# A decoder trunk on one core: the items of an attention head on 13 slots, and the projection's weight buffers opened inside the gate

## The chip, the cores and the metric

The kernel runs on one NeuronCore of a Trainium2 chip. The metric is the device time of one execution in microseconds. The engines are TensorE (PE in the profile, its weight loads PEld), VectorE (DVE), ScalarE (ACT), GpSimd (POOL), and SyncE (SP), which issues every DMA of this kernel.

## The reference, cut to what matters

Two layers work on 512 tokens of width 2048. Layer 0 is a pooling mixer, layer 1 sparse attention: an indexer scores the keys of each query, the best 128 are kept (as an additive mask here), and 16 heads of width 128 attend with it.

```python
proj = h @ w_in
q, k, v, gate, qi, ki, wi = jnp.split(proj, ATTN_SPLITS, axis=-1)
q = rope_partial(q.reshape(B, L, N_HEADS, HEAD_DIM), positions, ROT_DIM)
k = rope_partial(k.reshape(B, L, N_HEADS, HEAD_DIM), positions, ROT_DIM)
...
logits = jnp.einsum('bqhd,bqkhd->bhqk', qb, k_sel).astype(jnp.float32) * attn_scale
logits = jnp.where(valid[:, None], logits, -jnp.inf)
p = jax.nn.softmax(logits, axis=-1).astype(v.dtype)
return jnp.einsum('bhqk,bqkhd->bqhd', p, v_sel)
...
return (o * jax.nn.silu(gate)) @ w_out
```

Every layer's input is RMS-normed and modulated, its output is scaled by a gate from the conditioning vector and added to the residual.

## The kernel before

**Products.** All matmuls are of fp32r. An operand is split into a rounded part (ScalarE casts it, `hi`, `wh`, `qwh`) and the remainder (VectorE subtracts, `lo`, `wl`, `qwl`), and each product is three matmuls: hi·hi, hi·lo, lo·hi. So each unit of weights costs a load, a cast and a subtraction before TensorE can take it. `gemm_t` and `gemm_n` loop over eight steps `kp` of 256 rows of the contraction.

**Order of the work.** It is written out by hand. Two queues of closures hold the work beside the matmuls: `hot` and `bg`. After each step, `step(n, nhot)` runs `nhot` items of `hot` and, by a running debt, on average `n` items of `bg`; `mid={n: f}` calls f after the matmuls of step n, ahead of that `step`; `drain()` runs all that is left. The order in the program is a priority: the framework then lays down one fixed order for each engine, in which work that it expects to be ready can come ahead of earlier work that it expects to wait. A tile in a pool opened with `reuse_waits="tile"` waits for the readers of those tiles that lay at its place before.

**The gate.** After the indexer's projection, four chunks `c` of the gate are multiplied (L715, `gemm_t` over eight steps of 24 matmuls each, banks `acc`). `gate_evac` applies SiLU on ScalarE into `yst` (four buffers, in pool `yp`) and stores it to `yd` in DRAM. Meanwhile `bg` holds 8 `s_item` (sums and differences of `hT` into `SS`) and 54 top-k items (L655 on), which work on `score` in pool `ip`. Then `drain()` runs what is left of them, `yp`, `ip`, the work pools and the banks are closed, and the projection's pools `ap`, `wq` (its buffers `qst` x4, `qwh` x4, `qwl` x4, `t2` x4) and banks are opened.

**The projection.** For each pair of heads a = 2j, b = 2j+1, seven products P1 to P7 of a Strassen-like scheme replace eight: 28 slots `u` of 12 matmuls each (128x384), over the banks `bx`, `bz`, `by`. `qplan` orders them: slots 0 to 11 run P1, P5, P6 in turn, 12 to 19 P3 and P7, 20 to 27 P2 and P4. `q_unit` prepares the weights of a slot: it issues the loads up to `QAHEAD` = 2 units ahead, forms the sums that P5, P6, P7 and P4 need with VectorE (L760), and splits; it runs until `QLOOK` + 1 = 4 units are ready. After P7's last slot (19) the 11 items of head b are put on `bg`, after P4's last (27) those of head a, and each slot ends with `step(1)`: one item a slot. The first pair's slots also take 8 `s3_item` (differences of `hT`).

**The items of a head** (`head_items`): `rot_qk` rotates q and k (VectorE, last write L546), `turned` transposes q, then k (TensorE L825, cast, remainder), `keep_v` splits v and loads the stored gate, `soft(qb)` computes the scores of a block of queries (L849 to L851), adds the mask and takes the maximum (VectorE L854), and the exponential (ScalarE L857); `norm_p` divides (VectorE L863), `trans` transposes the probabilities (TensorE L869, cast and remainder into `ph`, `pl`), `pvs` multiplies by v (L880 to L882) and by the gate (L883). The PSUM tag `att`, which `turned`, `soft`, `trans` and `pvs` share, has two banks here. `vh`, `vl`, `ph`, `pl`, `na`, `nb` are single buffers.

**After the projection**, the first gemm of the output (L961) runs with `nstep=2.6, nhot=2, mid={6: drain}`; meanwhile the last items, and `y_split` for the 16 heads, come from `hot` and `bg`. Its step `kp` reads `yT` of heads 2kp and 2kp+1; the last pair is heads 14 (a) and 15 (b).

Of the kernel before, what the change touches and what calls it, by code (L numbers as in the profile page):

```python
# [9 lines left out]
F32 = mybir.dt.float32  # L10
# [4 lines left out]
PSUM = bass.MemoryType.PSUM  # L15
# [3 lines left out]
T = 512  # L19
# [14 lines left out]
NS = 3.4  # L34
NC = 1
# [19 lines left out]
def trunk(ctx, tc, xT, cols, crow, pos, modT, win, wgrp, wout0, widx, wgate, wqkv, wout1, out):  # L55
# [6 lines left out]
    P = {}  # L62
# [16 lines left out]
    ew = open_work("left")  # L79
    eb = open_banks()  # L80
# [53 lines left out]
    def drain():  # L134
        while hot:
            hot.popleft()()
        while bg:
            bg.popleft()()
# [41 lines left out]
    def gemm_t(kps, rhs, new_bank, evac, t0=0, t1=T, nstep=1, nhot=1, mid={}):  # L180
        banks = []
        for n, kp in enumerate(kps):
            wh, wl = next_unit()
            for m in range(4):
                if n == 0:
                    banks.append(new_bank())
                o = banks[m][:, 0:t1 - t0]
                for kk in range(2):
                    rh, rl = rhs(2 * kp + kk)
                    ms = slice(m * 128, m * 128 + 128)  # L190
                    first = n == 0 and kk == 0
                    last = n == len(kps) - 1 and kk == 1
                    mm(o, wh[:, kk, ms], rh[:, t0:t1], start=first, stop=False)  # L193
                    mm(o, wh[:, kk, ms], rl[:, t0:t1], start=False, stop=False)  # L194
                    mm(o, wl[:, kk, ms], rh[:, t0:t1], start=False, stop=last)  # L195
                if n == len(kps) - 1:
                    evac(m, o)
            if n in mid:
                mid[n]()
            step(nstep, nhot)  # L200
# [99 lines left out]
    hT = {}  # L300
# [22 lines left out]
    es = ExitStack()  # L323
# [128 lines left out]
    for g in range(4):  # L452
        pooled = {}
        for kk in range(4):
            k = 4 * g + kk
# [98 lines left out]

    er = ExitStack()
    sp = er.enter_context(tc.tile_pool(name="sp", bufs=1, side="right"))
    es = ExitStack()
    yp = es.enter_context(tc.tile_pool(name="yp", bufs=1))
    ip = es.enter_context(tc.tile_pool(name="ip", bufs=1))
# [12 lines left out]
    y = {}  # L572

    def y_tile(m):
        y[m] = yp.tile([128, T], F32, name="yst", tag="yst", bufs=4)

    for m, o in early_g:
        y_tile(m)
# [127 lines left out]
    def gate_evac(c, t0):  # L706
        def evac(m, o):
            mt = 4 * c + m
            if mt not in y:
                y_tile(mt)  # L710
            nc.scalar.activation(y[mt][:, t0:T], o, AF.Silu)
            nc.sync.dma_start(yd[mt], y[mt])
        return evac

    for c in range(4):  # L715
        t0 = 256 if c == 0 else 0
        gemm_t(range(8), lambda k: hT[k], bank4, gate_evac(c, t0), t0, T, nstep=NS if c > NC else 0.5)
    drain()
    es.close()
    ew.close()  # L720
    eb.close()

    QW = 384
    el = ExitStack()
    ap = el.enter_context(tc.tile_pool(name="ap", bufs=1, reuse_waits="tile"))
    wq = er.enter_context(tc.tile_pool(name="wq", bufs=1, side="right", reuse_waits="tile"))
    eq = ExitStack()
    P["ps"] = eq.enter_context(tc.tile_pool(name="pq", bufs=1, space=PSUM, reuse_waits="tile"))
    P["natt"] = 2


    qplan = []
# [21 lines left out]
    def q_unit():  # L754
        i = qpos[1]
        qpos[1] += 1
        q_loads(i + 1 + QAHEAD)
        prod, kp, _ = qplan[i]
        st = qraw.pop(i, None)
        sub = lambda o, x, z: nc.vector.tensor_tensor(o, x, z, op=OP.subtract)  # L760
        if prod == "P5":
            sub(st, st, was["b11"])
        elif prod == "P6":
            t2[kp] = wq.tile([128, 2, QW], F32, name=f"t2_{kp}")
            sub(t2[kp], st, was["t1"])
            st = t2[kp]
        elif prod == "P7":
            sub(st, was["b22"], st)
        elif prod == "P4":
            sub(t2[kp], was["b21"], t2[kp])  # L770
            st = t2[kp]
        keep = {"P1": "b11", "P5": "t1", "P3": "b22", "P2": "b21"}.get(prod)
        if keep:
            was[keep] = st
        wh = wq.tile([128, 2, QW], F32R, name="qwh", tag="qwh", bufs=QLOOK + 1)
        wl = wq.tile([128, 2, QW], F32R, name="qwl", tag="qwl", bufs=QLOOK + 1)
        split(wh, wl, st)
        qready.append((wh, wl))

    def lhs(prod, k, tt):  # L780
        ts = slice(tt * 128, tt * 128 + 128)
# [36 lines left out]
    def head_items(h, nat):  # L818
        x = nat.rearrange("p t (o d) -> p t o d", o=3)
        cell = {}  # L820

        def turned(s, nm):
            p = att()
            for tt in range(4):
                nc.tensor.transpose(p[:, tt * 128:tt * 128 + 128], x[:, tt, s, :], ident)  # L825
            a = ap.tile([128, T], F32R, name=nm + "h", tag=nm + "h")
            b = ap.tile([128, T], F32R, name=nm + "l", tag=nm + "l")
            split(a, b, p)
            cell[nm] = (a, b)

        def rot_qk():
            rope(ap, "rh", x[:, :, 0:2, 0:32], cosa, sina, [128, 4, 2, 32], 16)

        def keep_v():
            vh = ap.tile([128, 4, 128], F32R, name="vh", tag="vh")
            vl = ap.tile([128, 4, 128], F32R, name="vl", tag="vl")
            split(vh, vl, x[:, :, 2, :])
            cell["v"] = (vh, vl)
            cell["ph"] = ap.tile([128, 4, T], F32R, name="ph", tag="ph")
            cell["pl"] = ap.tile([128, 4, T], F32R, name="pl", tag="pl")  # L840
            cell["y"] = ap.tile([128, T], F32, name="yg", tag="yg", bufs=2)
            nc.sync.dma_start(cell["y"], yd[h])

        def soft(qb):
            n = (qb + 1) * 128
            (qh, ql), (kh, kl) = cell["q"], cell["k"]
            o = att()[:, 0:n]
            qs = slice(qb * 128, qb * 128 + 128)
            mm(o, qh[:, qs], kh[:, 0:n], start=True, stop=False)  # L849
            mm(o, qh[:, qs], kl[:, 0:n], start=False, stop=False)  # L850
            mm(o, ql[:, qs], kh[:, 0:n], start=False, stop=True)  # L851
            lg = ap.tile([128, n], F32, name="lg", tag="lg", bufs=3)
            st = ap.tile([128, 4], F32, name="stt", tag="stt", bufs=6)
            nc.vector.tensor_tensor_reduce(out=lg, in0=o, in1=mbias[qb], scale=1.0, scalar=GONE,  # L854
                                           op0=OP.add, op1=OP.max, accum_out=st[:, 0:1])
            nc.vector.tensor_scalar(st[:, 1:2], st[:, 0:1], -ATTN_SCALE, None, op0=OP.mult)
            nc.scalar.activation(lg, lg, AF.Exp, scale=ATTN_SCALE, bias=st[:, 1:2], accum_out=st[:, 2:3])  # L857
            cell["p", qb] = lg, st

        def norm_p(qb):  # L860
            lg, st = cell["p", qb]
            nc.vector.reciprocal(st[:, 3:4], st[:, 2:3])
            nc.vector.tensor_scalar(lg, lg, st[:, 3:4], None, op0=OP.mult)  # L863

        def trans(qb):
            lg, _ = cell["p", qb]
            p = att()
            for sb in range(qb + 1):
                nc.tensor.transpose(p[:, sb * 128:sb * 128 + 128], lg[:, sb * 128:sb * 128 + 128], ident)  # L869
            qs = slice(qb * 128, qb * 128 + 128)  # L870
            split(cell["ph"][:, 0:qb + 1, qs], cell["pl"][:, 0:qb + 1, qs],
                  p[:, 0:(qb + 1) * 128].rearrange("p (a b) -> p a b", b=128))

        def pvs():
            o = att()
            vh, vl = cell["v"]
            for sb in range(4):
                r = slice(sb * 128, T)
                ph, pl = cell["ph"][:, sb, r], cell["pl"][:, sb, r]
                mm(o[:, r], vh[:, sb, :], ph, start=sb == 0, stop=False)  # L880
                mm(o[:, r], vh[:, sb, :], pl, start=False, stop=False)
                mm(o[:, r], vl[:, sb, :], ph, start=False, stop=sb == 3)  # L882
            nc.vector.tensor_tensor(cell["y"], o, cell["y"], op=OP.mult)  # L883
            y[h] = cell["y"]
            if h < HEADS - 2:
                nc.sync.dma_start(yd[h], cell["y"])

        def at(*fs):
            def run():
                for f, *args in fs:  # L890
                    f(*args)
            return run

        return [at((rot_qk,)), at((turned, 0, "q")), at((turned, 1, "k")), at((keep_v,)), at((soft, 0)),
                at((soft, 1), (norm_p, 0)), at((soft, 2), (norm_p, 1), (trans, 0)),
                at((soft, 3), (norm_p, 2), (trans, 1)), at((norm_p, 3), (trans, 2)), at((trans, 3)), at((pvs,))]

    yT = {}

# [164 lines left out]
```

## Time and profile before

| | |
|---|---|
| median of 3 runs | 1688.88 us (1687.83 to 1691.62) |
| the profiled execution | 1691.16 us, its span in the trace 1689.4 us |
| TensorE busy | 1626.4 us, 96% of the span |
| VectorE busy | 1358.0 us, 80% |
| ScalarE busy | 717.6 us, 42% |
| mean granted clock of TensorE | 0.994 |

The gate ends at about 888 us, the projection runs from 896 to 1478 us. Matmuls overlap in the trace: each is recorded from its start to a modelled end, so the busy share says how seldom TensorE has nothing to do, and not how fast it works. In the rows, `PEclk` is the clock that was granted, 1.00 for 2.4 GHz and 0.50 for 1.2 GHz.

### The profile page before, as it was taken

How to read it: one execution, taken by the hardware profiler on the slowest of the kernel's cores; microseconds unless marked ns; L12 is line 12 of the kernel's file. 1: busy time of each engine (PE TensorE's matmuls, PEld its weight loads, DVE VectorE, ACT ScalarE, POOL GpSimd, SP SyncE). 2: the span in 40 equal slices, each digit the busy share in tenths (PEclk: the TensorE clock that was granted, in tenths of full speed). 3: DMA queues.
4: the chain of work that ended last, by engine and by line, in shares of the span. 5: the costliest groups of instructions: out<-in, count | busy, mean ns of one | idle time of the engine just before them, and what ended most of it. 6: DMA issues, size and time to landing. Idle time of an engine off the chain costs nothing.

```text
span 1689.4 us, 23722 instructions
## 1 busy us (share of the span) xinstructions
PE 1626.4 (96%) x8892; PEld 1461.7 (87%) x8892; DVE 1358.0 (80%) x2260; ACT 717.6 (42%) x1133; POOL 24.3 (1%) x130
## 2 busy tenths in 40 slices
PE   4999999999999999999998999999999999999997
PEld 2888888888889999998887999999999999978897
DVE  6899998999865689665978878888887888856754
ACT  4622221334224566454214544454544445544344
POOL 1000000000000000010000000000000000000000
PEclk9999999999999999999998999999999999999999
DMA  8888888444777775442326454444445444638854
GB/s 326 320 305 301 334 336 328 178 174 148 298 251 242 236 220 179 144 141 102 95 73 217 132 156 144 134 144 134 153 135 159 144 132 149 202 97 310 334 167 171
DMA packets 100772, 335.62 MB, mean 199 GB/s; under 512 B 11313, under 2 KB 19633, under 8 KB 88241
## 3 DMA queue, kind: packets, MB, share of 16 engines
q1 hardware_dynamic: 100658, 334.11, 57.1%
q8 instruction: 70, 1.15, 0.3%
q14 instruction: 44, 0.36, 0.1%
HBM read 317.81 MB, written 16.25 MB: 198 GB/s over the span
## 4 chain that ended last, share of the span: by engine, by line
PE 48%; issue 24%; DVE 15%; DMA 11%; ACT 1%; POOL 1%; DVEq 0%; POOLq 0%; SPq 0%; ACTq 0%
DMA qst<-wqkv 10%; PE acc L195 8%; PE acc L193 8%; PE acc L194 8%; DVE qwl L177 6%; PE att L195 4%; PE att L193 4%; PE att L194 4%; DVE t L760 2%; DVE qst L760 1%; PE acc L216 1%; PE acc L215 1%; PE acc L217 1%; PE by L804 1%; PE by L803 1%
## 5 line engine op out<-in xcount | busy, mean ns | idle before, releaser
L150 ACT CAST wh<-st 128x1024 fp32r<-128x1024 f32 (+1 forms) x232 | 236.2, 1018 | 497.4 <-PE acc L194 289.0
L152 DVE TENSOR_TENSOR wl<-st,wh 128x1024 fp32r<-128x1024 f32 (+1 forms) x232 | 273.9, 1181 | 137.1 <-ACT wh L150 135.1
L193 PE MATMUL acc<-hi,wh 128*128 128x512 f32 (+1 forms) x810 | 299.9, 371 | 0.0
L195 PE MATMUL acc<-hi,wl 128*128 128x512 f32 (+1 forms) x810 | 299.0, 369 | 0.4 <-DVE wl L152 0.4
L194 PE MATMUL acc<-lo,wh 128*128 128x512 f32 (+1 forms) x810 | 299.2, 369 | 0.0
L228 DVE SCALAR_TENSOR_TENSOR ms<-ms,cb 128x2048 f32<-128x2048 f32 x96 | 218.9, 2285 | 27.7 <-DMA ms<-modT 16.3
L176 ACT CAST qwh<-qst 128x768 fp32r<-128x768 f32 x160 | 133.6, 835 | 137.9 <-PE by L804 47.8
L195 PEld LDWEIGHTS acc<-hi,wl 128*128 128x128 f32 x810 | 152.5, 188 | 26.9 <-DVE wl L152 0.8
L194 PEld LDWEIGHTS acc<-lo,wh 128*128 128x128 f32 x810 | 152.8, 189 | 26.2
L193 PEld LDWEIGHTS acc<-hi,wh 128*128 128x128 f32 x810 | 152.7, 189 | 26.2
L177 DVE TENSOR_TENSOR qwl<-qst,qwh 128x768 fp32r<-128x768 f32 x160 | 151.4, 950 | 10.6 <-ACT qwh L176 10.5
L193 PE MATMUL att<-hi,wh 128*128 128x512 f32 (+1 forms) x406 | 148.3, 366 | 2.2 <-ACT hi L314 2.2
L194 PE MATMUL att<-lo,wh 128*128 128x512 f32 (+1 forms) x406 | 148.6, 366 | 0.0
L195 PE MATMUL att<-hi,wl 128*128 128x512 f32 (+1 forms) x406 | 148.2, 365 | 0.0
L802 PE MATMUL bx<-qwh,hi 128*128 128x384 f32 x256 | 89.5, 351 | 7.6 <-ACT qwh L176 7.6
L760 DVE TENSOR_TENSOR qst<-qst 128x768 f32<-128x768 f32 x64 | 61.1, 955 | 38.0 <-DMA qst<-wqkv 38.0
L193 PEld LDWEIGHTS att<-hi,wh 128*128 128x128 f32 x406 | 76.5, 189 | 15.1 <-ACT hi L314 2.6
L802 PE MATMUL by<-qwh,hi 128*128 128x384 f32 x256 | 87.3, 341 | 1.3 <-DVE nb L938 1.2
L194 PEld LDWEIGHTS att<-lo,wh 128*128 128x128 f32 x406 | 76.7, 189 | 13.4 <-DVE lo L315 0.8
L195 PEld LDWEIGHTS att<-hi,wl 128*128 128x128 f32 x406 | 76.7, 189 | 12.4
L803 PE MATMUL bx<-qwl,hi 128*128 128x384 f32 x256 | 87.0, 340 | 0.0
L804 PE MATMUL bx<-qwh,lo 128*128 128x384 f32 x256 | 86.8, 339 | 0.0
(285 smaller groups left out, 3478.4 us busy)
## 6 DMA issues: line engine op xcount, KB each, us to landing
ms<-modT SPq DMA_DIRECT2D x96, 1024.0 KB, 6.9
qst<-wqkv SPq DMA_DIRECT2D x192, 384.0 KB, 3.2
st<-wout SPq DMA_DIRECT2D x88, 512.0 KB, 4.2
st<-win SPq DMA_DIRECT2D x64, 512.0 KB, 4.7
st<-wgate SPq DMA_DIRECT2D x40, 512.0 KB, 3.5
st<-widx SPq DMA_DIRECT2D x32, 368.0 KB, 3.0
x<-xT SPq DMA_DIRECT2D x16, 256.0 KB, 5.4
st<-wgrp SPq DMA_DIRECT2D x8, 512.0 KB, 3.1
```

The source lines that it names most:

```text
L150: nc.scalar.copy(wh, st)
L152: nc.vector.tensor_tensor(wl, st, wh.bitcast(F32), op=OP.subtract)
L176: nc.scalar.copy(hi, src)
L177: nc.vector.tensor_tensor(lo, src, hi.bitcast(F32), op=OP.subtract)
L193: mm(o, wh[:, kk, ms], rh[:, t0:t1], start=first, stop=False)
L194: mm(o, wh[:, kk, ms], rl[:, t0:t1], start=False, stop=False)
L195: mm(o, wl[:, kk, ms], rh[:, t0:t1], start=False, stop=last)
L228: nc.vector.scalar_tensor_tensor(st, st, 1.0, cell["cb"], op0=OP.mult, op1=OP.mult, accum_out=dst)
L760: sub = lambda o, x, z: nc.vector.tensor_tensor(o, x, z, op=OP.subtract)
L802: mm(o, hi, wh[:, kk, :], start=first, stop=False, skip_group_check=not opens)
L803: mm(o, hi, wl[:, kk, :], start=False, stop=False, skip_group_check=not opens)
L804: mm(o, lo, wh[:, kk, :], start=False, stop=last, skip_group_check=not opens)
```

## The change

Two edits. First, `yst` gets a pool of its own, `ys`, opened below `yp`. `qplan`, `q_loads` and `q_unit` stand ahead of the gate's loop, and a new `q_open`, called by `mid` after the matmuls of step 5 (of 0 to 7) of the gate's last chunk, drains the queues, closes `yp` and `ip`, opens `wq` and prepares two units (which issues the loads of four). `t2` moves out of `wq` to a new pool `wt`, opened after the gate as `wq` was. Second, the items of a head are 13 instead of 11: `keep_v` comes second instead of fourth, the two `turned` one slot later, `trans(0)` moves from the slot of `soft(2)` to one of its own with `norm_p(2)`, `soft(3)`, `trans(1)`, `norm_p(3)` and `trans(2)` come one slot later each, then a slot is empty, and `trans(3)` and `pvs` come two slots later.

```diff
+    ey = ExitStack()
+    yst = ey.enter_context(tc.tile_pool(name="ys", bufs=1))
...
-        y[m] = yp.tile([128, T], F32, name="yst", tag="yst", bufs=4)
+        y[m] = yst.tile([128, T], F32, name="yst", tag="yst", bufs=4)
...
-    for c in range(4):
-        t0 = 256 if c == 0 else 0
-        gemm_t(range(8), lambda k: hT[k], bank4, gate_evac(c, t0), t0, T, nstep=NS if c > NC else 0.5)
-    drain()
-    es.close()
-    ew.close()
-    eb.close()
-
...
-    el = ExitStack()
-    ap = el.enter_context(tc.tile_pool(name="ap", bufs=1, reuse_waits="tile"))
-    wq = er.enter_context(tc.tile_pool(name="wq", bufs=1, side="right", reuse_waits="tile"))
...
-            t2[kp] = wq.tile([128, 2, QW], F32, name=f"t2_{kp}")
+            t2[kp] = wt.tile([128, 2, QW], F32, name=f"t2_{kp}")
...
+    def q_open():
+        nonlocal wq
+        drain()
+        es.close()
+        wq = er.enter_context(tc.tile_pool(name="wq", bufs=1, side="right", reuse_waits="tile"))
+        for _ in range(2):
+            q_unit()
+
+    for c in range(4):
+        t0 = 256 if c == 0 else 0
+        gemm_t(range(8), lambda k: hT[k], bank4, gate_evac(c, t0), t0, T, nstep=NS if c > NC else 0.5,
+               mid={5: q_open} if c == 3 else {})
+    ey.close()
+    ew.close()
+    eb.close()
+
+    el = ExitStack()
+    ap = el.enter_context(tc.tile_pool(name="ap", bufs=1, reuse_waits="tile"))
+    wt = er.enter_context(tc.tile_pool(name="wt", bufs=1, side="right", reuse_waits="tile"))
...
-        return [at((rot_qk,)), at((turned, 0, "q")), at((turned, 1, "k")), at((keep_v,)), at((soft, 0)),
-                at((soft, 1), (norm_p, 0)), at((soft, 2), (norm_p, 1), (trans, 0)),
-                at((soft, 3), (norm_p, 2), (trans, 1)), at((norm_p, 3), (trans, 2)), at((trans, 3)), at((pvs,))]
+        return [at((rot_qk,)), at((keep_v,)), at((turned, 0, "q")), at((turned, 1, "k")), at((soft, 0)),
+                at((soft, 1), (norm_p, 0)), at((soft, 2), (norm_p, 1)), at((trans, 0), (norm_p, 2)),
+                at((soft, 3), (trans, 1)), at((norm_p, 3), (trans, 2)), at(), at((trans, 3)), at((pvs,))]
```

## Rows read from the trace of the kernel before

**Rows 1.** The page, busy time, share of the span, instructions of one engine.

```profile
PE 1626.4 (96%) x8892; PEld 1461.7 (87%) x8892; DVE 1358.0 (80%) x2260; ACT 717.6 (42%) x1133; POOL 24.3 (1%) x130
```

**Rows 2.** Waits of TensorE, whole span: us in total, times, longest.

```profile
PE bx L802 <- ACT qwh L176: 7.6, 1, 7.6
...
PE att L869 <- DVE lg L863: 6.8, 14, 0.8
PE att L825 <- DVE nb L546: 5.7, 8, 0.9
PE att L849 <- DVE stt L854: 2.9, 7, 0.6
...
PE att L880 <- ACT ph L176: 2.4, 1, 2.4
...
PE by L802 <- DVE nb L938: 1.2, 1, 1.2
PE att L869 <- DVE stt L854: 1.1, 4, 0.4
```

**Rows 3.** Timeline of TensorE, gate's end: start, duration, instruction [idle before, releaser].

```profile
887.95 0.39 PE L195 MATMUL acc<-hi,wl 128*128 128x512 f32 x1
895.96 1.01 PE L802 MATMUL bx<-qwh,hi 128*128 128x384 f32 x2 [7.62 <-ACT qwh L176]
...
902.24 0.35 PE L802 MATMUL bz<-qwh,s1h 128*128 128x384 f32 x1
...
903.29 0.33 PE L802 MATMUL by<-qwh,s2h 128*128 128x384 f32 x1
...
905.38 0.34 PE L802 MATMUL bx<-qwh,hi 128*128 128x384 f32 x1
```

**Rows 4.** Busy time: stretch, us, PE, PEld, DVE, ACT, POOL, PEclk, DMA, GB/s.

```profile
888.00:896.00 8.00, 0.38 (x3) 0.04 (x1) 4.97 (x13) 3.33 (x8) 0.00 (x0) 0.75 0.80 265
900.00:902.00 2.00, 2.00 (x8) 2.00 (x8) 2.00 (x3) 0.57 (x1) 0.00 (x0) 0.50 0.84 263
903.29:911.64 8.35, 8.35 (x49) 8.35 (x49) 8.18 (x12) 4.37 (x6) 0.00 (x0) 1.00 0.65 200
```

**Rows 5.** Timeline of VectorE around the gate's end.

```profile
872.56 0.42 DVE L669 TENSOR_SCALAR mbias<-score 128x512 f32<-128x512 f32 x1
...
889.30 0.76 DVE L177 TENSOR_TENSOR lo<-lg,hi 128x256 fp32r<-128x256 f32 x2 [12.68 <-ACT hi L176]
...
896.81 0.95 DVE L760 TENSOR_TENSOR qst<-qst 128x768 f32<-128x768 f32 x1
```

**Rows 6.** Timeline of the DMA queue, same stretch.

```profile
849.65 11.44 SPq L148 DMA_DIRECT2D st<-wgate  x3
...
891.63 12.97 SPq L750 DMA_DIRECT2D qst<-wqkv  x9
```

**Rows 7.** What the DMA queue waited for, 888 to 900 us.

```profile
SPq L750 <- DMA yd<-yst: 1.7, 1, 1.7
```

**Rows 8.** Timeline of ScalarE around the gate's end.

```profile
888.87 0.70 ACT L176 CAST hi<-lg 128x256 fp32r<-128x256 f32 x2
...
895.07 0.83 ACT L176 CAST qwh<-qst 128x768 fp32r<-128x768 f32 x1 [1.70 <-DMA qst<-wqkv]
```

**Rows 9.** Timeline of TensorE, a stretch of the projection.

```profile
1313.84 0.34 PE L803 MATMUL by<-qwl,hi 128*128 128x384 f32 x1
1314.95 0.63 PE L825 MATMUL att<-ident,nb 128*128 128x128 f32 x4 [0.77 <-DVE nb L546]
```

**Rows 10.** Busy time in a stretch of the first output gemm.

```profile
1490.00:1495.00 5.00, 5.00 (x22) 4.31 (x21) 2.96 (x6) 1.87 (x3) 0.00 (x0) 0.72 0.33 105
```

**Rows 11.** Timeline of VectorE, end of the last head.

```profile
1521.37 0.69 DVE L883 TENSOR_TENSOR yg<-att,yg 128x512 f32<-128x512 f32 x1 [2.01 <-PE att L882]
1522.74 0.69 DVE L177 TENSOR_TENSOR lo<-yg,hi 128x512 fp32r<-128x512 f32 x1 [0.69 <-ACT hi L176]
```

**Rows 12.** Timeline of ScalarE, same stretch.

```profile
1522.09 0.62 ACT L176 CAST hi<-yg 128x512 fp32r<-128x512 f32 x1 [4.11 <-DVE yg L883]
```

More of the change, by code (lines that the diff above doesn't have):

```diff
@@ L713, in gate_evac @@
         return evac
-    for c in range(4):
-        t0 = 256 if c == 0 else 0
-        gemm_t(range(8), lambda k: hT[k], bank4, gate_evac(c, t0), t0, T, nstep=NS if c > NC else 0.5)
-    drain()
-    es.close()
-    ew.close()
-    eb.close()
-    QW = 384
-    el = ExitStack()
-    ap = el.enter_context(tc.tile_pool(name="ap", bufs=1, reuse_waits="tile"))
-    wq = er.enter_context(tc.tile_pool(name="wq", bufs=1, side="right", reuse_waits="tile"))
-    eq = ExitStack()
-    P["ps"] = eq.enter_context(tc.tile_pool(name="pq", bufs=1, space=PSUM, reuse_waits="tile"))
-    P["natt"] = 2
+    QW = 384
+    wq = None
     qplan = []
@@ L778, in q_unit @@
         qready.append((wh, wl))
+    def q_open():
[15 more added lines that the diff above has]
+    wt = er.enter_context(tc.tile_pool(name="wt", bufs=1, side="right", reuse_waits="tile"))
+    eq = ExitStack()
+    P["ps"] = eq.enter_context(tc.tile_pool(name="pq", bufs=1, space=PSUM, reuse_waits="tile"))
+    P["natt"] = 2
     def lhs(prod, k, tt):
```

## The prediction

> **What bounds the kernel.** I read four views in this order. The page first: TensorE is busy for 96% of the span [rows 1], so a change can win only where TensorE waits or where its clock is low. Then the waits of TensorE alone, over the whole span [rows 2]: apart from what stands before and after the stages touched here, they are one wait of 7.6 us where the projection starts, 34 short ones inside the projection (6.8 + 5.7 + 2.9 + 1.2 + 1.1 = 17.7 us), and one of 2.4 us in the first output gemm. Then the timelines of the engines around the first of these [rows 3 to 8], and last a short stretch of the projection and the tail [rows 9 to 12]. The edits reach all three places, so each gets a sum of its own.
>
> **Opening the weight buffers early.** The gate's last matmul starts at 887.95, and since these follow each other every 0.23 us the engine is free at 888.18; the projection's first starts at 895.96 [rows 3]. That is 7.78 us. After it the clock is at its lower level: the granted clock in 900 to 902 is 0.50 (1.2 GHz), from 903.29 on 1.00 (2.4 GHz) [rows 4]. From 895.96 to 902.24 there are 18 matmuls in 6.28 us; a slot of 12 at full clock takes 903.29 to 905.38, 2.09 us [rows 3], so the 18 would take 3.13 us. The restart loses another 3.15 us, together 10.9 us.
>
> Why it waits: the weight loads are issued only from 891.63 on [rows 6], and what their line waited for on the queue is the landing of a store of `yd` from `yst` [rows 7]; that is, the new buffer lies where `yst` lay. Before that the queue has nothing of the projection, though the gate's last three loads were issued between 849.65 and 861.09. The change takes `yst` out of the way and puts the loads of four units (and the splits of two) before the last two steps of the gate. What they overwrite then is the indexer's workspace. VectorE's last reading of it, the mask, is at 872.56 [rows 5], 15 us before the gate ends. The ten top-k items that `drain` now issues at once are therefore no cost: VectorE has run ahead of TensorE and is through with them. Nor do the early loads hit others, since those of the gate are out by 861.
>
> What stays of the 10.9 us: (1) the PSUM bank of the projection's first product is free once the gate's evacuation has run; ScalarE is done with the last of four at about 888.9, when its next work starts [rows 8], so 0 to 0.8 us; I take 0.4. (2) `t2`, needed by the third unit, moves to a pool that opens only after the gate and by the sizes of the tiles lies over `yst` now; its subtraction may wait for the same store, until about 891.6, and then a subtraction, a cast and a split follow, 0.95 + 0.83 + about 0.95 us [rows 5, 8], while the third slot would start at 888.2 + 2 x 2.09 = 892.4. Its first matmul needs the cast, at 893.4: 1.0 us, with the split up to 2.0, or 0 if the overlapping buffer is stored earlier. I take 1.2. (3) VectorE used the old gap: 4.97 us of work in 888 to 896 [rows 4], mostly the hT differences. Afterwards it is busy for 8.18 of 8.35 us [rows 4], so there is no room to do this later at no cost. Two operations (0.95 us each) now come before the gate's end, so at most 3.1 us of delay, at least nothing, as units are split up to three slots ahead; I take 1.5. Sum of the three 3.1, bounds 0 and 5.9. If the buffer is free early the gap no longer lowers the clock. Gain 10.9 - 3.1 = **7.8 us**, between 5 and 10.9.
>
> **The 13 slots.** The idle column is no true price. In [rows 9] TensorE's idle time before the transpose is 0.77 us, but from the start of the matmul before it to its own start are 1.11 us, where 0.17 is usual: 0.94 lost. Each matmul is recorded 0.34 us long and the next starts after 0.17, so a stall costs its idle time and 0.17 more. The 34 waits cost 17.7 + 34 x 0.17 = 23.5 us. The Trainium skill (Perfetto Trace Analysis, Identifying the Most-Contended Engine) says that matmul busy time misleads on how near TensorE is to its limit, because matmuls overlap; by the busy time itself the ceiling would be 17.7, by the starts it is 23.5, and these rows side with the starts.
>
> By kind [rows 2], each with 0.17 for every wait: (b) transposes of the probabilities that wait for their normalisation, 14, 6.8 + 2.4 = 9.2 us. The last key block was: scores, then normalisation one slot on, transpose the next. It becomes scores, one on, then two on. A slot of 2.09 us covers the 0.66 us a time. I leave 0.6. (c) The last scores, which wait for the reduction of the scores before them to free a bank, 7, 4.1 us: one slot apart before, two now, with only one transpose between. I leave 0. (a) The first transpose of an odd head, waiting for its rotation, 8, 7.1 us. The list puts `keep_v` between, which looks like a slot; but in [rows 9] the transpose already stands behind 11 of the slot's 12 matmuls, so it moves by one matmul, 0.17 us. I leave 5.7, bounds 1 and 7. (d) Transposes waiting for the reduction of the last scores, 4, 1.8 us. These two items stay one slot apart, and stalls removed before them bring TensorE here sooner on both heads: I leave 4, bounds 1 and 8. (e) The wait for an evacuation, 1.4 us, stays. Left: 0.6 + 0 + 5.7 + 4 + 1.4 = 11.7. Gain 23.5 - 11.7 = **11.8 us**, bounds 5 and 19. The matmuls themselves are as many as before.
>
> **The tail.** Two heads are now 26 items in 28 slots instead of 22, so 17 instead of 13 are left for the first output gemm, with two `y_split`. Its steps pop 3, 3, 2, 3, 2, 3 (2.6 a step on the rest that all earlier steps leave). Before, all 15 were out after the sixth; now the last head's `pvs` and both splits come with the `drain` after the seventh, and the eighth step starts with the head that they make. In the kernel before, the chain behind `pvs` is a product at 1521.37 [rows 11], a cast from 1522.09 to 1522.71 [rows 12] and the remainder, done at 1523.43 [rows 11]: 1.34 and 2.06 us, and with the hand-over from TensorE some 1.5 to the first matmul that can go, 2.2 to the second. The next gemm's matmuls may stand in. Loss 0 to 2.2, I take 1.0. On the other side is the wait of 2.4 us for `ph` [rows 2]. The first `pvs` of this gemm met it two items after its transpose's step began; it is now a step later than its transpose. That wait costs 2.4 + 0.17, and the clock falls after it, to a mean of 0.72 in 1490 to 1495 [rows 10], which is 56% of 5 us at the lower level, 1.4 us lost. Together 4.0; I count 70% of it, 2.8. Net gain **1.8 us**, bounds -2.2 and 4.0.
>
> **Sum.** 7.8 + 11.8 + 1.8 = 21.4 us from the profiled execution's 1691.16 (span 1689.4, 1.8 around it) is 1669.8. That execution lay 2.3 above the median of the runs, 1688.88, so the likeliest time is between 1667.5 and 1669.8; I say 1668.
>
> **Rivals.** R1, chance 0.58: as summed. R2, 0.15: the early opening gives little, because VectorE's displaced work, `t2`'s wait and a second clock loss eat it: the speaking row is VectorE's 8.18 of 8.35. Then 1 to 3 instead of 7.8: about 1674. R3, 0.15: the respacing mostly moves the waits: 34 short ones have VectorE at their end, whose amount of work is unchanged, and (a) and (d) keep their distance. Then 3 instead of 11.8: about 1677. R4, both at once or the changed order never reaching the engines' queues, 0.06: 1684 to 1689.
>
> R5, 0.06, slower. `keep_v` is two slots earlier, and its cast of `vh`, a single buffer, must wait for the last head's `pvs`. ScalarE takes its queue in order: VectorE stands still for 12.68 us, up to 889.30, for a cast whose input it had written before [rows 5], and that cast starts only at 888.87, behind the gate's evacuations [rows 8]. So if the cast is queued ahead of that `pvs`, all weight casts behind it are late. The code leaves two slots, 4.2 us, between them, and casts run three slots ahead, so it decides only from a block of some 6.3 us. Then each of 14 heads would lose a slot, 14 x 2.09 = 29 us, against the gains of 21.4: 1689 + 8 = 1697. The Trainium skill (PSUM — Partial Sum Buffer, Engine vs sequencer instructions) states the rule, that ScalarE's and VectorE's queues are strictly first in, first out; the row agrees.
>
> **Numbers.** A measurement of this kernel tells about 0.2%, 3.4 us, from no change. R1 to R3 end faster, and a part of R4; faster 0.89, same 0.05, slower 0.06. R2 and R3 reach to 1677 with their own spread of some 5, and the good ends of the three terms (10.9, 19, 3) to 1656; I leave out R4, R5 and the joint best: 1658 to 1682.
>
> **What would show it.** Right: the weight loads issued before 880; first projection matmul within 1 us of the gate's last, clock 1.00 throughout; waits of TensorE in the projection under 9 us in sum, none of the transposes on the normalisation, but those on the rotation still there; no `ph` wait near the tail, a short one before the last step of the first output gemm. Wrong: a wait of more than 2.5 us in the first slots with a clock of 0.5 behind it (R2), as many short waits under other names (R3), or TensorE waiting for `qwh` in every pair while ScalarE waits for `pvs` (R5).

## The result, and the profile after

The changed kernel takes 1664.9 us (median of 4 runs, 1664.35 to 1665.37), the kernel before on the same chip 1690.18 us (4 runs). The ratio is 0.9852, its 95% interval 0.9835 to 0.9869: 25.3 us faster, where the prediction said 1668 us and 21.4 us. The profiled execution has a span of 1663.6 us against 1689.4. Of all executions reported below one is slow and left out (3271.86 us, of the run with `t2` reversed).

The page of the changed kernel, busy time by engine, which answers to [rows 1]: TensorE's busy time has fallen by 5 us only, the span by 26; VectorE's has not fallen at all.

```profile
PE 1621.0 (97%) x8892; PEld 1459.2 (88%) x8892; DVE 1358.2 (82%) x2260; ACT 717.5 (43%) x1133; POOL 24.2 (1%) x130
```

The waits of TensorE over the whole span (us in total, times, longest), which answer to [rows 2]:

```profile
PE att L882 <- DVE pl L177: 3.7, 6, 1.5
...
PE att L894 <- DVE pl L177: 1.8, 8, 0.2
...
PE by L815 <- ACT qwh L176: 1.0, 1, 1.0
...
PE att L838 <- DVE nb L546: 0.6, 1, 0.6
```

The lines have moved: L815 to L817 are the projection's matmuls, L838 the transposes of q and k, L862 to L864 the scores, L882 the transposes of the probabilities, L893 to L895 the value products. Of the kinds (a) to (e) only one wait of (a) is left. In their place stand two that were not in the trace before: the second transposes of the probabilities (`trans(1)`) and the value products now wait for `pl`, the remainder that VectorE writes from the transposes before them. The list has one more wait, of 0.2 us, released by L875, the reciprocal of `norm_p`: it stands ahead of a `trans(1)`, right behind the remainder of `trans(0)`, so it goes with the new kind and not with (d), whose releaser was the reduction of the scores (L854 before, L867 now).

The timeline of TensorE where the gate ends (start, duration, instruction, idle time before it and its releaser), which answers to [rows 3]:

```profile
888.87 0.39 PE L195 MATMUL acc<-hi,wl 128*128 128x512 f32 x1
889.09 0.34 PE L815 MATMUL bx<-qwh,hi 128*128 128x384 f32 x1
...
893.11 0.34 PE L817 MATMUL bz<-qwh,s1l 128*128 128x384 f32 x1
894.46 0.62 PE L815 MATMUL by<-qwh,s2h 128*128 128x384 f32 x2 [1.02 <-ACT qwh L176]
...
1456.65 0.48 PE L193 MATMUL acc<-hi,wh 128*128 128x512 f32 x1
```

The projection's first matmul follows the gate's last after 0.22 us, the pitch of the gate's own. The only loss is at the third unit: 1.35 us from start to start where 0.17 is usual, 1.18 lost. The last row is the first matmul of the output, at 1456.65; in the kernel before it starts at 1478.29.

The same stretch by engine (the columns of [rows 4]) shows the full clock, where before it fell to 0.50:

```profile
888.00:896.00 8.00, 6.75 (x35) 5.59 (x33) 4.51 (x9) 4.43 (x8) 0.00 (x0) 1.00 0.63 224
896.00:900.00 4.00, 4.00 (x23) 4.00 (x24) 4.00 (x7) 1.33 (x2) 0.00 (x0) 1.00 0.56 189
1490.00:1495.00 5.00, 5.00 (x25) 4.01 (x24) 2.99 (x8) 1.88 (x5) 0.00 (x0) 1.00 0.16 39
```

The third of them answers to [rows 10]: 1.00 instead of 0.72. The work in these 5 us is not the same, since everything is some 22 us earlier; but the clock is 1.00 in the whole of 1456 to 1515, and no wait for `ph` is left.

SyncE's, VectorE's and ScalarE's timelines explain the 1.18 us. Five loads of the projection go out from 862.09 on, the last by 877.2, 14 us and more ahead of [rows 6]; the gate's last store goes out at 889.92; VectorE's first subtraction into `t2` waits for it, and ScalarE's cast for that subtraction:

```profile
862.09 15.10 SPq L739 DMA_DIRECT2D qst<-wqkv  x5
885.84 3.04 SPq L714 DMA_DIRECT2D yd<-yst  x3
...
889.92 0.32 SPq L714 DMA_DIRECT2D yd<-yst  x1
```

```profile
892.59 0.96 DVE L749 TENSOR_TENSOR t<-qst 128x768 f32<-128x768 f32 x1 [1.27 <-DMA yd<-yst]
```

```profile
893.58 0.83 ACT L176 CAST qwh<-t 128x768 fp32r<-128x768 f32 x1 [1.83 <-DVE t L749]
```

By stages, from the starts in the two timelines (the projection is counted to the first output matmul at 1478.29 and 1456.65, and its first row here is without the restart at the low clock and without the 1.18):

| stage | before | after | gain | predicted |
|---|---|---|---|---|
| opening (gap, low clock, third unit) | 10.93 | 1.18 | 9.75 | 7.8 |
| rest of the projection | 579.18 | 566.37 | 12.8 | 11.8 |
| first output matmul to the end | 211.11 | 206.95 | 4.2 | 1.8 |
| up to the gate's end | 888.18 | 889.10 | -0.9 | 0 |

They sum to 25.8 us, the difference of the two spans. This is one trace on either side; how far single traces of one kernel differ stands at the end of the next section.

### The profile page after: what moved, and what is told of

Read it like the earlier page. It is cut to its first block, busy times and chain, and to the rows that moved or that the text cites. A ratio compares the mean times of both kernels' runs of the same rounds, so it can differ in the third digit from the quotient of the medians.

```text
span 1663.6 us, 23680 instructions
## 1 busy us (share of the span) xinstructions
PE 1621.0 (97%) x8892; PEld 1459.2 (88%) x8892; DVE 1358.2 (82%) x2260; ACT 717.5 (43%) x1133; POOL 24.2 (1%) x130
## 4 chain that ended last, share of the span: by engine, by line
PE 62%; issue 24%; DVE 9%; DMA 3%; ACT 1%; POOL 1%; POOLq 0%; SPq 0%; DVEq 0%; ACTq 0%
PE acc L194 8%; PE acc L195 8%; PE acc L193 8%; PE att L194 4%; PE att L195 4%; PE att L193 4%; DVE qwl L177 3%; PE by L815 3%; PE by L816 3%; PE by L817 3%; DMA qst<-wqkv 2%; PE bx L815 2%; PE bx L817 2%; PE bx L816 2%; PE bz L816 1%
## 5 line engine op out<-in xcount | busy, mean ns | idle before, releaser
L815 PE MATMUL bx<-qwh,hi 128*128 128x384 f32 x256 | 88.6, 347 | 0.1
L815 PE MATMUL by<-qwh,hi 128*128 128x384 f32 x256 | 88.4, 345 | 0.0
L176 ACT CAST qwh<-t 128x768 fp32r<-128x768 f32 x64 | 53.6, 837 | 77.7 <-PE by L817 47.6
L817 PE MATMUL bx<-qwh,lo 128*128 128x384 f32 x256 | 86.1, 336 | 0.0
```

The lines of the kernel that those rows point to most:

```text
L176: nc.scalar.copy(hi, src)
L815: mm(o, hi, wh[:, kk, :], start=first, stop=False, skip_group_check=not opens)
L817: mm(o, lo, wh[:, kk, :], start=False, stop=last, skip_group_check=not opens)
```

## Experiments

**The two edits apart.** The first run (e1) is the changed kernel with the list of 11 back; the second (e2) is the kernel before with the list of 13.

```diff
@@ e1
+        return [at((rot_qk,)), at((turned, 0, "q")), at((turned, 1, "k")), at((keep_v,)), at((soft, 0)),
+                at((soft, 1), (norm_p, 0)), at((soft, 2), (norm_p, 1), (trans, 0)),
+                at((soft, 3), (norm_p, 2), (trans, 1)), at((norm_p, 3), (trans, 2)), at((trans, 3)), at((pvs,))]
```

> The opening alone, on the kernel before: the gate's hook, the places of yst and t2, and the old list of 11 items. If the parts are independent (theory), the opening keeps what the two traces show of it, 10.9 us of loss turned into 1.2: about 9.75 us under the kernel before, 1680 us, TensorE's clock 1.00 through the first slots of the projection, and in the projection all of the waits of before (transposes on the normalised rows 9.2, on the rotation 7.1, scores on ScalarE 4.1). Rival: a share of the 12.8 us of the projection comes from the earlier start of the loads, so this run gains 12 to 15 us and the waits of the projection shrink without the new list.

> The list over 13 slots alone, with the opening of before. Theory, parts independent: the projection and the tail give 12.8 + 4.2 = 17 us less 0.9, so 1673 to 1674 us, with the gap of 7.78 us and the low clock still at the gate's end. Rival, the earlier loads carry a share of it: 5 to 10 us only, and transposes still wait for the rotation.

Measured: the opening alone 1681.02 us, ratio 0.9939 (0.9918 to 0.9959); the list alone 1673.13 us, ratio 0.9896 (0.9877 to 0.9916); the kernel before beside them 1691.83. The product of the two ratios is 0.9836, and the whole change measures 0.9852 (0.9835 to 0.9869): within the intervals the parts add. By stages too: the rest of the projection and the tail take 579.9 and 210.3 us with the opening alone (before 579.2 and 211.1), 566.0 and 206.1 with the list alone (changed kernel 566.4 and 207.0), where 1.18 us of opening is taken off the one and 10.9 off the other. The waits say the same. With the opening alone TensorE still waits in the projection as before (the scores' waits, which the expectation puts down to ScalarE, are for VectorE's reduction):

```profile
PE att L882 <- DVE lg L876: 6.4, 14, 0.5
PE att L838 <- DVE nb L546: 5.4, 8, 0.9
PE att L882 <- DVE stt L867: 3.3, 7, 1.0
PE att L862 <- DVE stt L867: 2.9, 5, 0.7
PE att L893 <- ACT ph L176: 2.2, 1, 2.2
```

With the list alone they are gone but for three short ones (1.6 us in all), and the gap of 7.6 us at the gate's end stays:

```profile
PE bx L802 <- ACT qwh L176: 7.6, 1, 7.6
PE att L881 <- DVE pl L177: 3.5, 9, 1.4
PE att L869 <- DVE pl L177: 2.6, 4, 1.3
```

**What in the opening counts: the place of a buffer or the place in the program?** Two runs on the changed kernel. One calls `q_open` behind the gate's loop; the other does that too and puts `yst` back into `yp`, so that of the opening only `t2`'s own pool remains.

```diff
@@ both
-               mid={5: q_open} if c == 3 else {})
+               mid={})
+    q_open()
@@ the second also
-    ey = ExitStack()
-    yst = ey.enter_context(tc.tile_pool(name="ys", bufs=1))
-        y[m] = yst.tile([128, T], F32, name="yst", tag="yst", bufs=4)
+        y[m] = yp.tile([128, T], F32, name="yst", tag="yst", bufs=4)
```

> The changed kernel with the opening's code behind the gate's last product instead of inside it (yst still has a place of its own, t2 its new pool). Theory 'position': SyncE's queue then holds the gate's stores, which wait for the last Silu, ahead of the projection's loads; the loads land after the gate's end and 6 to 10 us of the 9.75 are lost again: 1671 to 1675 us. Rival 'place': what mattered was that the loads had to wait for the bytes of yst to be stored; with yst elsewhere they start within about 1 us of where they do in the changed kernel, and the time is within 2 us of 1665.

> The late opening of the run before, with yst back in the pool yp as in the kernel before; of the opening only t2's own pool, opened after wq, is left. Theory: moving t2 out of wq does not by itself take wq off the bytes of yst; the loads wait for the stores again, the gap of 7.6 us and the low clock return, and the time is 1674 to 1676 us. Rival: with t2's 12 kB out of it wq no longer reaches yst, the loads go out early, and the time is within 2 us of 1666; then yst's pool of its own was needed only for the program's order.

Measured: 1666.2 us for the late call (ratio 0.9851, the changed kernel's 0.9852), 1675.78 us with `yst` back (ratio 0.9889). The changed kernel beside the second of them takes 1667.11, so `yst` in its old place costs 8.7 us. My theory on the position fell: a call behind the loop costs nothing. SyncE's timeline of that run shows why: the framework's fixed order has put the loads ahead of the gate's stores by itself, as soon as nothing made them wait.

```profile
862.65 15.09 SPq L739 DMA_DIRECT2D qst<-wqkv  x5
886.39 3.04 SPq L714 DMA_DIRECT2D yd<-yst  x3
```

With `yst` back in its old place the loads go out at 890.59, and TensorE's first projection matmul waits again, with the clock at 0.50 in 898 to 902:

```profile
896.46 1.01 PE L813 MATMUL bx<-qwh,hi 128*128 128x384 f32 x2 [7.42 <-ACT qwh L176]
```

So the opening's gain, all of it that these times can tell (8.7 us here, 9.75 in the traces), comes from the bytes: the first weight buffers no longer lie over `yst`.

**The 1.18 us at the third unit.** The four `t2` buffers are laid out in reverse order.

```diff
+    for kp in reversed(range(4)):
+        t2[kp] = wt.tile([128, 2, QW], F32, name=f"t2_{kp}")
...
-            t2[kp] = wt.tile([128, 2, QW], F32, name=f"t2_{kp}")
```

> The changed kernel with the four t2 buffers laid out in the reverse order, so that the first to be written lies at the other end of their pool. Theory: the loss of 1.18 us at the third slot is t2's wait for the last store of yst; then VectorE's first t2 subtraction waits for no store, the TensorE wait on qwh there is gone, and 1.2 us are gained (1663.7 us on the chip where the changed kernel takes 1664.9). Rival: all of the pool lies over yst buffers that are stored as late, or VectorE is late there anyway: no change.

Measured: 1664.79 us (1662.0 to 1668.35) where the changed kernel takes 1667.11 beside it, 2.3 less, but the runs of each spread over 6 to 8 us there, so the times do not settle 1.2. The trace does: no wait of TensorE is left between 888.5 and 898, and the same subtraction starts without one.

```profile
890.91 0.95 DVE L749 TENSOR_TENSOR t<-qst 128x768 f32<-128x768 f32 x1
```

**Why the waits for the rotation went.** The prediction left 5.7 of 7.1 us there; 0.8 were left. One run (e4) is the kernel before with the value item in second place, nothing else; the other (e8) is the changed kernel with the value item behind the k transpose and its old slot empty.

```diff
@@ e4, on the kernel before
-        return [at((rot_qk,)), at((turned, 0, "q")), at((turned, 1, "k")), at((keep_v,)), at((soft, 0)),
+        return [at((rot_qk,)), at((keep_v,)), at((turned, 0, "q")), at((turned, 1, "k")), at((soft, 0)),
@@ e8, on the changed kernel
-        return [at((rot_qk,)), at((keep_v,)), at((turned, 0, "q")), at((turned, 1, "k")), at((soft, 0)),
+        return [at((rot_qk,)), at(), at((turned, 0, "q")), at((turned, 1, "k"), (keep_v,)), at((soft, 0)),
```

> The kernel before, its list of 11 items with the value item moved from fourth to second place and nothing else. The q and k transposes then stand one slot later, as in the list of 13. Theory: that one slot alone ends the transposes' wait for the rotation (7.1 us with the pitch's share), so about 6 to 7 us are gained, 1682 to 1684 us, and the other waits of the projection stay. Rival: the distance was the same one matmul that my prediction counted, and the wait vanished in the changed kernel since VectorE is less behind when it comes to the rotation; then 5 of the 8 waits or more stay here, and the time is 1687 to 1689 us.

> The changed kernel's list of 13 with the value item put back behind the k transpose (same slot as it) and an empty slot in its old place, so that rotation and q transpose keep their distance. Theory: the waits for the rotation vanished in the changed kernel because the value item's cast and remainder went early and no longer stand among the rotation's operations on VectorE; then 5 or more of the 8 waits for the rotation return, 3 to 5 us, and the time is 1668 to 1670 us where the changed kernel takes 1665. Rival: they vanished because the whole list is spaced wider and VectorE waits less for loads (29.5 us in the changed kernel, 64.1 before, 43.9 with the value item moved alone); then at most 2 waits for the rotation show, VectorE's waits for loads stay at 25 to 35 us, and the time is within 2 us of the changed kernel.

Measured: e4 1684.89 us, ratio 0.9962 (0.9948 to 0.9977), about 6.4 us faster than the kernel before beside it (1691.83); e8 1664.2 us where the changed kernel takes 1664.85 beside it. In e4 the rotation's waits stay, 7 of 8, 3.8 us and with 0.17 each 5.0 (7.1 before), and a new kind comes beside them:

```profile
PE att L825 <- DVE nb L546: 3.8, 7, 0.8
PE att L850 <- DVE kl L177: 3.7, 9, 1.0
```

So one slot is one matmul, as the prediction counted: before, 11 of the slot's 12 matmuls stand ahead of the transpose, in e4 all 12. The 2.1 us so gained are the smaller part of e4's 6.4; the waits for the scores' reduction (2.9) and for the evacuation (1.2) are gone too. My theory for e4 fell. Its rival held for the waits, but not for the time: it had 1687 to 1689 us, since it did not see that the other kinds would go.

In e8 no wait for the rotation shows, as its rival said, but the run decides little: in its trace ScalarE's order in the projection is that of the changed kernel, and so is VectorE's around every rotation. The framework laid the value item's work where the changed kernel has it. What speaks against the value item is in other rows. Before and in e4 its remainder `vl` stands ahead of the rotation's last write in seven pairs of eight. In the last pair it stands behind, and the transpose waits all the same, 0.76 and 0.80 us. And in the changed kernel a weight split of 0.95 us has the place of `vl` (0.69) in six pairs; the rotation takes longer there from its first operation to its last, 2.04 us against 1.76, and is early nevertheless. VectorE and TensorE in the last pair of the kernel before:

```profile
1461.01 0.42 DVE L546 TENSOR_TENSOR nb<-rt,rt 128x256 f32<-128x256 f32 x1
...
1462.21 0.68 DVE L177 TENSOR_TENSOR vl<-nb,vh 128x512 fp32r<-128x512 f32 x1
```

```profile
1461.57 0.63 PE L825 MATMUL att<-ident,nb 128*128 128x128 f32 x4 [0.76 <-DVE nb L546]
```

So VectorE comes earlier to the rotation, and what brings it there is the wider list: with the list alone (e2), too, one wait of 0.6 is left. VectorE's waits for loads go with it: 64.1 us before (38.0 + 26.1), 43.9 in e4, 30.0 in e2, 29.5 in the changed kernel, 27.3 in e8.

How the list does it is not shown; one reading of the traces is this. When the value products of a head are done, `yg` is stored to `yd`. The framework's order has the loads of `yg` two heads ahead (the first two go out beside the gate's stores), so the next one goes into the buffer that this very store must leave: SyncE waits for the landing (28.1 us in 14 waits before), and every weight load behind it in the queue waits too. In the kernel before, SyncE's and VectorE's timelines around the rotation whose write ends at 1241.03:

```profile
1222.87 0.33 SPq L886 DMA_DIRECT2D yd<-yg  x1
1226.38 0.33 SPq L842 DMA_DIRECT2D yg<-yd  x1
1227.61 20.29 SPq L750 DMA_DIRECT2D qst<-wqkv  x8
```

```profile
1231.12 1.93 DVE L760 TENSOR_TENSOR t<-qst,t 128x768 f32<-128x768 f32 x2 [0.77 <-DMA qst<-wqkv]
...
1240.61 0.42 DVE L546 TENSOR_TENSOR nb<-rt,rt 128x256 f32<-128x256 f32 x1
```

From that late load on VectorE has no pause until the rotation is done, 0.14 us before the transpose that waited for it. The changed kernel stores 9 us before this transpose instead of 18 (1215.51 against 1224.54), so the block falls behind the loads that the rotation's neighbours need, and the rotation is done 1.17 us ahead of TensorE. Its amount is not what changed: SyncE waits for these landings for 32.2 us in 14 waits in the changed kernel, more than before. That its place made the difference was not tried (a third `yg` buffer would tell). And the first pair, which has no store ahead of it, waits for its rotation before and after (0.55 and 0.56 us); the last VectorE work of `s3_item` ends over 20 us ahead of it, so this wait stays unexplained.

**The waits that came instead.** In e6 the empty slot is used to part `trans(1)` from `soft(3)`; in e11 and e12 lists of 14, with `t2` reversed, part the value products from their transposes too (the last lines of each list).

```diff
@@ e6
+                at((soft, 3)), at((norm_p, 3), (trans, 1)), at((trans, 2)), at((trans, 3)), at((pvs,))]
@@ e11
+                at((soft, 3)), at((trans, 1), (norm_p, 3)), at((trans, 2)), at((trans, 3)), at(), at((pvs,))]
@@ e12
+                at((soft, 3), (trans, 1)), at((norm_p, 3), (trans, 2)), at(), at((trans, 3)), at(), at((pvs,))]
```

> The changed kernel with the empty slot used: trans(1) and trans(2) each one slot later, each in a slot without another user of a bank before it. Theory: the new waits of the changed kernel, transposes on the remainder pl (3.7 us in 6 and with the pitch 4.7) and the value products on pl (1.8 in 8, 3.2), come from trans(1) standing right behind soft(3) with two banks; the first kind goes, the second, which follows trans(3), stays: 4 to 5 us gained, 1660 to 1661. Rival: trans(2), trans(3) and pvs, now in three slots in a row, get the wait instead: within 2 us of the changed kernel.

> The changed kernel with t2 in reverse order and a list of 14: trans(1), trans(2), trans(3) in slots of their own behind the last scores, then an empty slot, then the value products; two heads fill all 28 slots. Theory: the waits on pl (5.5 us and 2.4 of the pitch) go, and with t2's 1.2 it takes 1657 to 1659 us where the changed kernel takes 1665, if the two items that the tail gets more cost nothing. Rival: VectorE, 82% busy, only moves its lateness, as in the run with the empty slot used: within 3 us of the changed kernel.

> The changed kernel with t2 in reverse order and a list of 14, the changed list with one more empty slot ahead of the value products. Theory: the wait of the value products on pl goes (1.8 us and 1.4 of the pitch), that of trans(1) on pl stays, t2's 1.2 is gained: 1661 to 1662 us where the changed kernel takes 1665. Rival: the tail, which gets two items more, pays 2 us or more for them: 1664 us or above.

Measured: e6 1665.73 us beside 1667.11, no difference that the times can tell. Its waits moved as the rival said, from the second transposes to the value products: 6.7 us in 9 (1.8 in 8 before).

```profile
PE att L894 <- DVE pl L177: 6.7, 9, 1.2
```

The lists of 14 are slower than the changed kernel (1664.85 beside them) by 18 and 14 us: 1682.64 (ratio to before 0.9948) and 1679.26 (0.9918). Neither theory had this. The waits on `pl` are gone in e11 and down to 1.3 us in e12, but a larger one stands at the first scores, once a head:

```profile
PE att L865 <- DVE kl L177: 18.6, 14, 3.3
```

The projection takes 581.1 us in e11 instead of 567.6 and the tail 209.7 instead of 207.0. The longest of these waits in e11, by SyncE, VectorE and TensorE:

```profile
1116.88 0.33 SPq L901 DMA_DIRECT2D yd<-yg  x1
1121.20 0.33 SPq L857 DMA_DIRECT2D yg<-yd  x1
1121.62 6.93 SPq L739 DMA_DIRECT2D qst<-wqkv  x3
```

```profile
1122.26 0.68 DVE L177 TENSOR_TENSOR ql<-att,qh 128x512 fp32r<-128x512 f32 x1
1126.37 0.96 DVE L749 TENSOR_TENSOR qst<-qst 128x768 f32<-128x768 f32 x1 [3.42 <-DMA qst<-wqkv]
1127.24 0.95 DVE L177 TENSOR_TENSOR qwl<-qst,qwh 128x768 fp32r<-128x768 f32 x1
1128.11 0.68 DVE L177 TENSOR_TENSOR kl<-att,kh 128x512 fp32r<-128x512 f32 x1
```

```profile
1128.85 0.33 PE L865 MATMUL att<-kl,qh 128*128 128x128 f32 x1 [3.30 <-DVE kl L177]
```

Store and reload follow each other, 4.32 us apart; the weight load behind them goes out at 1121.62, VectorE stands 3.42 us for it, that unit's split and `kl` stand behind, and TensorE waits 3.30. In the changed kernel VectorE reaches the `kl` of the same head at 1119.08, 0.54 us before the scores begin:

```profile
1116.54 0.68 DVE L177 TENSOR_TENSOR ql<-att,qh 128x512 fp32r<-128x512 f32 x1
1118.20 0.96 DVE L177 TENSOR_TENSOR qwl<-t,qwh 128x768 fp32r<-128x768 f32 x1 [0.98 <-ACT qwh L176]
1119.08 0.68 DVE L177 TENSOR_TENSOR kl<-att,kh 128x512 fp32r<-128x512 f32 x1
```

Two things differ, then, and the runs do not part them. One is VectorE's fixed order: between `ql` and `kl` stand a subtraction that needs a load and that unit's split, in 15 of 16 heads in e11 and 14 in e12 (in e11 13 of these subtractions wait for the load, 0.49 to 3.42 us); in the changed kernel only one of the two stands there in 13 heads. The other is where the loads fall. That store and reload have no load between them is not enough: so it is in 7 of 14 pairs of the changed kernel, up to 5.0 us apart, as here, where TensorE's next transpose of q does not wait:

```profile
1215.51 0.33 SPq L899 DMA_DIRECT2D yd<-yg  x1
1219.69 0.33 SPq L855 DMA_DIRECT2D yg<-yd  x1
```

And in the first such pair of e11 a weight load does go out between them (969.71, behind the store at 968.24), and TensorE waits 2.65 us for `kl` nevertheless.

The Trainium skill (DMA: Bandwidth & Descriptors, Rules for kernel authors) asks that a DMA which reads what an earlier one wrote be issued only after the first one's completion has been waited for. Here the second one writes where the first one reads, a case that the rule does not name; SyncE waits for the landing there too, and since it issues everything else, the weight loads behind wait with it (3.5 us from 1222.87 to 1226.38 in the kernel before, 4.3 in e11).

**The changed kernel again**, beside the last two sets.

> The changed kernel itself, beside the others on the same chip: 1664 to 1666 us.

> The changed kernel itself, beside the others on the same chip: 1663 to 1667 us.

Measured: 1667.11 (1663.04 to 1671.35) and 1664.85 us (1664.49 to 1667.34), ratios 0.9839 and 0.9835. In three traces of this one program the projection takes 567.6, 572.7 and 568.3 us, so a difference of 5 us between single executions says nothing by itself. The one of 572.7 has longer waits on `pl` (8.7 us instead of 5.5), and behind two of them, of 1.94 and 2.09 us, the granted clock is 0.50 for some 3 us. No version tried here beats the changed kernel by more than that.

## Why the prediction was right, point by point

**The opening, right in place, a little small.** The three terms that it left were 0.4 for the PSUM bank, 1.2 for `t2` and 1.5 for VectorE's displaced work. Measured: 0, 1.18 and 0. The bank is no wait at all; `t2` waits for the store as the prediction worked out, and with the buffers reversed it does not. The displaced work was mis-sized: VectorE is busy for 4.00 of 4 us in 896 to 900, but units are split ahead, and no wait of TensorE follows. Rival R2 fell with that, and R4 with the two runs that part the edits: either one shows in the traces and the times.

**The 13 slots, right in sum, by errors that cancel.** (b) and (c) went as said: 9.2 and 4.1 us to nothing. (e), 1.4, which I kept, is gone as well. (d) was mis-sized: 4 left, none measured. (a) is the step that failed: "it moves by one matmul, 0.17 us. I leave 5.7". The matmul was counted rightly, and with that alone (e4) 5.0 are left; but I took VectorE's and SyncE's side as unchanged, and with the whole list 0.8 are left. That VectorE comes earlier is shown, by what is only read. Against this stand two kinds that I had not foreseen, both on `pl`: 3.7 + 6 x 0.17 = 4.7 and 1.8 + 8 x 0.17 = 3.2 us, and the 0.4 (0.2 and the pitch) of one more. `trans(1)` stands behind `soft(3)` and `trans(0)` with two banks, so its bank is free only when VectorE has written the remainder of `trans(0)`; I could have read that from the new list. Left were 9.1 us by these rows (0.8 + 0.4 + 4.7 + 3.2), 11.7 predicted. That would be 14.4 gained where the stage shows 12.8; the rest lies within what single traces differ by. So the nearness of 12.8 to 11.8 is luck: the terms missed by more, in both directions. Rival R3 named this mechanism; it needed 20.5 us left in all.

**The tail, mis-sized.** 4.2 us gained, 1.8 predicted, with 4.0 as the upper bound; in the other two traces of the changed kernel the tail takes 208.2 and 206.1 us, a gain of 2.9 and 5.0. The wait for `ph` went, with the clock's fall behind it; the loss of 1.0 before the last step did not come, since the next gemm's matmuls stand in, as the prediction allowed. TensorE's timeline right behind the last value products:

```profile
1504.36 0.44 PE L193 MATMUL att<-hi,wh 128*128 128x512 f32 x1
...
1506.13 0.96 PE L193 MATMUL acc<-hi,wh 128*128 128x512 f32 x3
```

Seven matmuls of the next gemm into `att` bridge the 1.8 us until `acc` goes on.

The low end of the range was summed with 3 for the tail, not with this bound; that moves it by 1 us and changes nothing here.

**R5**, a cast of `vh` that blocks ScalarE, is there but too small to cost: ScalarE stands for the value products ahead of that cast in 7 heads, 10.4 us in all and at most 1.6 (7.4 in 7 before), where the prediction asked for some 6.3 at once. No wait of TensorE for `qwh` is left in the projection but the one of the third unit.

## What to carry to other kernels

A load that must wait for a store to leave its buffer holds up every load behind it on the same queue (28.1 us in 14 waits in the kernel before). Whether that costs anything depends on what stands behind: before respacing work, look in each engine's fixed order which operation that needs a late load comes ahead of one that TensorE needs soon. A gap where a stage begins can be a matter of bytes: see which buffer the first load of the new stage overwrites before moving code, since here the framework moved the issue by itself once nothing held it. An edit of the program's order may not reach the engines at all; compare their orders in the trace before reading the time. And more room is not always better: 11 to 13 slots gained 13 us in the projection, 14 lost all of that again.

## What the runs showed of the hardware that I had not expected

TensorE's clock falls behind pauses of a few us, and the length of the pause alone does not say whether it will. In e11 (columns of [rows 4]) the granted clock was 0.50, 1.2 GHz, behind pauses of 2.65 us (first matmul behind it at 979.39) and 3.30 us (1128.85). Behind one of 1.70 us, at 1054.60, it stayed at 1.00; behind one of 1.67 us, at 1421.49, it fell to 0.50 as well, 1.5 us after the matmuls had gone on. In e4 it stayed at 1.00 behind 2.43 us (1481.88).

```profile
980.00:982.00 2.00, 2.00 (x8) 2.00 (x8) 1.32 (x4) 0.49 (x2) 0.00 (x0) 0.50 0.44 167
1055.30:1057.30 2.00, 2.00 (x14) 2.00 (x13) 1.65 (x6) 0.54 (x3) 0.00 (x0) 1.00 0.46 174
1423.50:1425.50 2.00, 2.00 (x9) 2.00 (x8) 0.85 (x2) 0.55 (x1) 0.00 (x0) 0.50 0.55 146
```

All three stretches show TensorE fully busy, with 8 and 9 matmuls in 2 us at the low clock and 14 at the full one. The wait column gives the pause alone; what follows it at half speed is lost on top.
